# Layer 0's mixer in another order: keys and first queries before values, the last GLU pair after the fourth scores, and new planned waits

## The chip, the cores and the metric

The kernel runs on one core of a Trainium2 chip. The metric is device time of one launch, in microseconds; lower is better. It is given as the median of three runs. Beside it stands one profiled execution, from which all durations below are read.

## The reference

A decoder trunk of two layers over 512 tokens of width 1024, in float32. Each layer adds a token mixer and then a SwiGLU block to the residual, each behind an RMS norm. The change lies in layer 0's mixer, whose parts are these:

```
proj = h @ w_in                      # 1024 -> 1792: q (8 heads), k, v (2 heads), glu (2 x 512)
q, k = rotary(q), rotary(k)
a    = band_attention(q, k, v, window 127, sinks)        # 128-token blocks, own and previous block
c    = g_a * sigmoid(g_b)
c    = silu(layer_norm(causal_depthwise_conv(c, width 31)))
h    = h + concat(a, c) @ w_out
```

Layer 1's mixer (a dilated attention beside a spatial gating unit) and the two SwiGLU blocks keep their code; layer 1 shares two of the edited lines.

## The kernel before

Activations lie transposed, as eight tiles `xs[k]` of 128 channels by 512 tokens. Each float32 product is made of three TensorE (PE) matmuls of 128x512 on a high and a low half of both operands (`acc3`, L198 to L204). The halves of the weights are made on the fly: ScalarE (ACT) copies a tile's high half (`w_hi`, L174) and GpSimd (POOL) subtracts for the low half (`w_lo`, L151) while layer 0's mixer runs. Four such units are in flight, so POOL makes the next ones only as PE uses up the old ones.

**Steps.** The mixer is a list of steps, `C0["steps"]` (L40), that the loop at L681 walks: `k`, `v`, `q0` to `q3` are column tiles of the input projection, `gN` is a pair of them (`a` and `b`) for the GLU, `SN` and `VN` are scores and values of head pair N, `L` the convolution's layer norm. `A`, `X`, `Y`, `B`, `C` are pieces of the output projection: `A`, `X` and `Y` use attention tiles 0 to 3, `B0`, `B3` and `C12` use the four normed convolution tiles.

**PE's order is planned by hand.** `Seq` (L208) keeps a clock `seq.t`. Every `acc3` advances it by a fixed price (L204, L265). S, V and L are generators that yield (cost, wait); they are resumed between two `acc3` when their wait is over on that clock. So the numbers in `C0` (`q` before the first scores, `S` between halves of a score step, `ST` from scores to values, `TA` for a copy, `AO` for the normalised output, `ln` the clock time of the four transposes of the layer norm) set where in PE's stream each small step stands. PE runs that stream strictly in order; if an operand isn't there, all of PE waits. `seq.until` (L236) jumps the clock forward where a step has nothing left to run beside. The other engines' queues are ordered by the scheduler, and run in order too.

**GLU and convolution.** Once pair N is projected, VectorE (DVE) multiplies both halves (`glu`, L494), writing the padded tile `cp[N]` (`cp_124` to `cp_127` in the rows). Then `conv_tile` (L467) makes 31 taps: the first `taps[N]` go to POOL (ACT multiplies into `prod`, three buffers, L478; POOL adds into `yc`, L479), the others to DVE (L481, L483). A last DVE add joins both (L484). `yc_136` to `yc_139` are the four results.

**Layer norm.** `conv_norm` (L633) transposes each `yc` on PE into bank 7 (L641), takes statistics on DVE, then scales, transposes back (L668), applies Silu on ACT and splits in halves; only then `B0` can start.

**Scores and values.** `scores0` (L573) runs 16 small matmuls in two halves into banks 2 and 3; DVE masks and reduces (L598), ACT takes exponentials (L610). `values0` and `pt_av` (L620, L395) transpose the weights into banks 4 and 7, ACT copies them (`pts`, L410), PE multiplies by `Vt` (L421), DVE scales by `rl` (`on`, L430), PE transposes again (L435), and ACT and DVE split the result into `oh` and `ol` (L363, L364).

Of the kernel before, what the change touches and what calls it, by code (L numbers as in the profile page):

```python
# [10 lines left out]
def _warn_once_fixed(msg, *args, **kwargs):  # L11
# [13 lines left out]
S = 512  # L25
# [9 lines left out]
C0 = dict(  # L35

    first='a0 b0',
    steps='L g0 v q0 g1 k S0 q1 S1 V0 g2 q2 q3 S2 V1 g3 S3 V2 V3 A1 A0 A2 Y5 X1 A3 Y6 X3 X0 X2 Y7 B0 B3 C12',  # L40
    na=(0, 1), nx=(2, 3, 4),
    rope_v=('k', 'q2', 'q3'),
    taps=(8, 15, 15, 10),

    norm=(0.0, 2.6), q=5.99, v=0.5, S=3.13, ST=0.86, TA=0.65, AO=1.09, LB=4.85, LO=2.1, ln=(54.8, 69.91, 96.75, 112.86),

    n1=5, q1=6.6, S1=2.26, ST1=3.65, m1=11.78, M1=0.53, TA1=1.12, AO1=1.4,
)
# [86 lines left out]
def trunk_kernel(ctx: ExitStack, tc: tile.TileContext, xT, ws, cols, sinks, sgu_g, sgu_b,  # L135
# [11 lines left out]
    def bank(i, shape=None):  # L147
        return psum.tile(shape or [P, S], F32, name=f"bank{i}")
# [49 lines left out]
    def acc3(ps, x, start, stop):  # L198
        hi, lo = next_tile()
        xh, xl = x  # L200
        T.matmul(ps, hi, xh, start=start, stop=False)  # L201
        T.matmul(ps, hi, xl, start=False, stop=False)  # L202
        T.matmul(ps, lo, xh, start=False, stop=stop)  # L203
        seq.tick(0.648)  # L204

# [35 lines left out]
    seq = Seq()  # L243
# [7 lines left out]
    def tok_gemm(x, banks, each=None, hold=0, ready=None):  # L251

        ps = [bank(b) for b in banks]
        last = len(x) - 1

        def mac(t, k, row):
            hi, lo = row
            xh, xl = x[k]  # L260
            c = slice(t * P, (t + 1) * P)
            T.matmul(ps[t], xh[:, c], hi, start=(k == 0), stop=False)  # L262
            T.matmul(ps[t], xh[:, c], lo, start=False, stop=False)  # L263
            T.matmul(ps[t], xl[:, c], hi, start=False, stop=(k == last))  # L264
            seq.tick(0.648)  # L265

        for k in range(len(x) - hold):
            row = next_row()
            for t in range(NQ):
                mac(t, k, row)  # L270
            if each:
                each(k)
        if hold:
            rows = {k: next_row() for k in range(len(x) - hold, len(x))}
            for t in range(NQ):
                for k, row in rows.items():
                    mac(t, k, row)
                ready(t, ps[t])
        return ps
# [34 lines left out]
    norm = {}  # L314
# [80 lines left out]
    def pt_av(items, vap, rl, dst, banks, line="V", ta="TA", ao="AO"):  # L395

        po = bank(5, [P, 8, 64])
        turn = [0]

        def tbank():  # L400
            turn[0] += 1
            return bank(banks[turn[0] % len(banks)])

        def trans(grp):
            pt = tbank()
            for x, (u, pap, blk, first, last) in enumerate(grp):
                T.transpose(pt[:, x * P:(x + 1) * P], pap, ident)
            pts = mpool[0].tile([P, S], F32, name="pts", bufs=3)
            w = len(grp) * P
            A.activation(pts[:, :w], pt[:, :w], AF.Copy)  # L410
            return pts

        grps = [items[c:c + 4] for c in range(0, len(items), 4)]
        pts, at = {}, {}
        for g in range(min(2, len(grps))):
            pts[g] = trans(grps[g])
            at[g] = seq.t + 0.43 + C0[ta]
            yield 0.43, (0.0 if g == 0 else max(0.0, at[0] - seq.t - 0.43))
        for g, grp in enumerate(grps):
            for x, (u, pap, blk, first, last) in enumerate(grp):  # L420
                T.matmul(po[:, u, :], pts[g][:, x * P:(x + 1) * P], vap(u, blk), start=first, stop=last)  # L421
            cost = 0.43
            if g + 2 < len(grps):
                pts[g + 2] = trans(grps[g + 2])
                at[g + 2] = seq.t + 0.86 + C0[ta]
                cost = 0.86
            if g + 1 < len(grps):
                yield cost, max(0.0, at[g + 1] - seq.t - cost)
        on = mpool[0].tile([P, NQ, P], F32, name="on", bufs=1)
        V.tensor_mul(on.rearrange("p n (b e) -> p (n b) e", b=2), po,  # L430
                     rl[:, :, None].to_broadcast([P, 8, 64]))
        yield 0.43, C0[ao]
        pt = tbank()
        for n in range(NQ):
            T.transpose(pt[:, n * P:(n + 1) * P], on[:, n, :], ident)  # L435
        split(pt, oh_[0][dst], ol_[0][dst])
        done.add((line, dst))
        yield 0.43, 0.0
# [5 lines left out]
    with ExitStack() as mx:  # L444
# [126 lines left out]
        oh_[0], ol_[0] = oh, ol  # L571

        def scores0(i):  # L573
            yield 0.0, C0["q"]
            while i >= 2 and ("V", i - 2) not in done:
                yield 0.0, 0.3
            qss = qTs[i][1]
            Pm = mp.tile([P, 8, 2 * P], F32, name="Pm", bufs=2)
            nm = scr.tile([P, 8], F32, name="nm")
            l = scr.tile([P, 8], F32, name="l")  # L580
            for n2 in range(2):
                sb = [bank(2), bank(3)]
                for n1 in range(2):
                    n = 2 * n2 + n1
                    for b in range(2):
                        lo = max(n - 1, 0) * P
                        w = (n + 1) * P - lo
                        out = sb[b][:, n1 * 256 + 256 - w:n1 * 256 + 256]
                        q = slice(n * P, (n + 1) * P)
                        T.matmul(out, qss[b][:, q], khh[b][:, lo:lo + w], start=True, stop=False)  # L590
                        T.matmul(out, qss[b][:, q], kl[b][:, lo:lo + w], start=False, stop=True)
                for n1 in range(2):
                    n = 2 * n2 + n1
                    for b in range(2):
                        u = 2 * n + b
                        c0 = P if n == 0 else 0
                        hd = i + 4 * b
                        V.tensor_tensor_reduce(  # L598
                            out=Pm[:, u, c0:], in0=sb[b][:, n1 * 256 + c0:n1 * 256 + 256],
                            in1=mask0[:, c0:], scale=-0.125, scalar=nsink[:, hd:hd + 1],  # L600
                            op0=ALU.add, op1=ALU.min, accum_out=nm[:, u:u + 1])
                if n2 == 0:
                    yield 0.9, C0["S"]
            es = scr.tile([P, 8], F32, name="es")
            V.tensor_tensor(out=es.rearrange("p (n b) -> p n b", b=2),
                            in0=nm.rearrange("p (n b) -> p n b", b=2),
                            in1=sinkb[:, i:i + 5:4][:, None, :].to_broadcast([P, NQ, 2]), op=ALU.add)
            for u in range(8):
                c0 = P if u < 2 else 0
                A.activation(Pm[:, u, c0:], Pm[:, u, c0:], AF.Exp, bias=nm[:, u:u + 1], scale=-1.0,  # L610
                             accum_out=l[:, u:u + 1])
            A.activation(es, es, AF.Exp)
            rl = scr.tile([P, 8], F32, name="rl")
            V.tensor_add(rl, l, es)
            V.reciprocal(rl, rl)
            del qTs[i]
            pend[i] = Pm, rl, seq.t + 0.9 + C0["ST"]
            yield 0.9, 0.0

        def values0(i):  # L620
            while i not in pend:
                yield 0.0, 0.3
            Pm, rl, at = pend.pop(i)
            yield 0.0, max(0.0, at - seq.t)
            items = []
            for u in range(8):
                n, b = divmod(u, 2)
                if n:
                    items.append((u, Pm[:, u, 0:P], n - 1, True, False))
                items.append((u, Pm[:, u, P:], n, n == 0, True))  # L630
            yield from pt_av(items, lambda u, blk: Vt[:, blk, 64 * (u % 2):64 * (u % 2) + 64], rl, i, (4, 7))

        def conv_norm():  # L633

# [1 line left out]
            bs = scr.tile([P, NQ, 4, 6], F32, name="bs")  # L636
            for j in range(4):
                yield 0.0, max(0.0, C0["ln"][j] - seq.t)
                pt = bank(7)
                for t in range(NQ):  # L640
                    T.transpose(pt[:, t * P:(t + 1) * P], yc[j][:, t * P:(t + 1) * P], ident)  # L641
                for t in range(NQ):
                    V.bn_stats(bs[:, t, j, :], pt[:, t * P:(t + 1) * P])
                A.activation(y[:, :, j * P:(j + 1) * P], pt.rearrange("p (t c) -> p t c", t=NQ), AF.Copy)
                yield 0.43, 0.0
# [32 lines left out]
                yield 0.43, (C0["LO"] if 0 < j < 3 else 0.0)  # L678

        qTs, pend, po, ks, early = {}, {}, {}, {}, {}  # L680
        for step in C0["steps"].split():  # L681
            kind, i = step[0], int(step[1:] or 0)
            if kind == "g":
# [658 lines left out]
```

## Time and profile before

| | |
|---|---|
| median of three runs | 1114.96 us (1112.4 to 1115.18) |
| profiled execution | 1111.7 us |
| span of its instructions | 1110.0 us |
| PE busy over the span | 1069.4 us (96%) |
| DVE, ACT, POOL busy | 694.0, 571.6, 233.2 us |

Layer 0's mixer takes the first 200 us or so. A timeline row reads: start, duration, engine, line, operation, output and inputs, count, and in brackets the idle time just before it with what ended it. Busy time of PE counts overlapping matmuls; the pace of dense 128x512 matmuls is read from the starts.

### The profile page before, as it was taken

To read this page: it belongs to the slowest core of one execution; us is meant where nothing else is said; L and a number is where in the kernel's file an instruction comes from. 1 tells how busy PE (TensorE), PEld (TensorE's weight loads), DVE (VectorE), ACT (ScalarE), POOL (GpSimd) and SP (SyncE) were. 2 spreads that over 40 slices of the span, in tenths; PEclk is the share of its full clock that TensorE was granted. 3 is DMA by queue.
4 is the path that set the end of the run, shared out by engine and by line. 5 is a ranking of instruction groups with operands and counts; after the bars stand their busy time and mean duration, and the time that the engine had idled before them with its cause. 6 is when DMAs were issued, how large, how long until landed. Compare 5 with 4: busy or idle time off the path is not lost.

```text
span 1110.0 us, 13707 instructions
## 1 busy us (share of the span) xinstructions
PE 1069.4 (96%) x5118; PEld 886.8 (80%) x5118; DVE 694.0 (63%) x1059; ACT 571.6 (51%) x930; POOL 233.2 (21%) x210
## 2 busy tenths in 40 slices
PE   9988889999999999999999999999899999999997
PEld 7767777878888888888887888888788888888785
DVE  3899965876565655564748646666765646555543
ACT  6577756754445353543637654446544443535433
POOL 0799744211101010100024200002110110101002
PEclk9999899999999999999999999999999999999999
DMA  6221112987757676621522112239877676766112
GB/s 228 68 76 58 39 38 76 285 210 192 181 160 169 181 150 198 144 47 57 160 98 83 41 43 72 77 106 269 207 194 188 154 172 185 140 197 143 29 67 76
DMA packets 42803, 145.89 MB, mean 131 GB/s; under 512 B 4848, under 2 KB 5744, under 8 KB 42736
## 3 DMA queue, kind: packets, MB, share of 16 engines
q1 hardware_dynamic: 30496, 100.88, 26.4%
q0 software_dynamic: 11520, 41.95, 22.3%
q10 hardware_dynamic: 720, 2.18, 0.6%
q8 instruction: 40, 0.66, 0.2%
q14 instruction: 27, 0.22, 0.1%
HBM read 142.89 MB, written 2.10 MB: 131 GB/s over the span
## 4 chain that ended last, share of the span: by engine, by line
PE 77%; DVE 10%; DMA 4%; ACT 4%; issue 3%; POOL 2%; POOLq 0%; ACTq 0%; DVEq 0%
PE bank L201 11%; PE bank L202 10%; PE bank L907 10%; PE bank L203 10%; PE bank L908 10%; PE bank L905 10%; DMA raw<-in_ws 4%; PE bank L262 2%; PE bank L264 2%; PE bank L263 2%; DVE bank L483 2%; PE bank L421 2%; PE bank L920 1%; DVE w2l L151 1%; ACT w2h L881 1%
## 5 line engine op out<-in xcount | busy, mean ns | idle before, releaser
L151 DVE TENSOR_TENSOR w2l<-raw,w2h 128x1024 fp32r<-128x1024 f32 x140 | 171.2, 1225 | 204.8 <-ACT w2h L881 200.5
L881 ACT ACTIVATE w2h<-raw 128x1024 fp32r<-128x1024 f32 x140 | 147.8, 1059 | 210.8 <-PE bank L908 159.0
L174 ACT ACTIVATE w_hi<-raw 128x512 fp32r<-128x512 f32 x204 | 127.7, 628 | 178.3 <-PE bank L202 141.2
L871 POOL DMA_DIRECT2D raw<-in_ws x80 | 69.6, 876 | 551.6 <-DVE w2l L151 229.7
L151 DVE TENSOR_TENSOR w_lo<-raw,w_hi 128x512 fp32r<-128x512 f32 x164 | 115.9, 710 | 57.1 <-ACT w_hi L174 57.0
L907 PE MATMUL bank<-w2l,s 128*128 128x512 f32 x320 | 125.0, 391 | 2.7 <-DVE w2l L151 2.7
L905 PE MATMUL bank<-w2h,s 128*128 128x512 f32 x320 | 125.6, 393 | 1.5 <-DVE gb L841 1.3
L908 PE MATMUL bank<-w2h,s 128*128 128x512 f32 x320 | 124.7, 390 | 0.0
L201 PE MATMUL bank<-xh,w_hi 128*128 128x512 f32 x272 | 110.0, 404 | 1.1 <-ACT w_hi L174 1.1
L203 PE MATMUL bank<-xh,w_lo 128*128 128x512 f32 x272 | 106.8, 393 | 0.0
L202 PE MATMUL bank<-xl,w_hi 128*128 128x512 f32 x272 | 106.7, 392 | 0.0
L201 PE MATMUL bank<-hh,w_hi 128*128 128x512 f32 x256 | 99.8, 390 | 0.0
L202 PE MATMUL bank<-hl,w_hi 128*128 128x512 f32 x256 | 99.7, 390 | 0.0
L203 PE MATMUL bank<-hh,w_lo 128*128 128x512 f32 x256 | 99.7, 389 | 0.0
L905 PE MATMUL bank<-w2h,xh 128*128 128x512 f32 x240 | 94.4, 393 | 0.0
L908 PE MATMUL bank<-w2h,xl 128*128 128x512 f32 x240 | 93.5, 390 | 0.0
L907 PE MATMUL bank<-w2l,xh 128*128 128x512 f32 x240 | 93.4, 389 | 0.0
L907 PEld LDWEIGHTS bank<-w2l,s 128*128 128x128 f32 x320 | 60.1, 188 | 16.3 <-DVE w2l L151 4.1
L905 PEld LDWEIGHTS bank<-w2h,s 128*128 128x128 f32 x320 | 60.1, 188 | 15.0 <-DVE gb L841 1.7
L908 PEld LDWEIGHTS bank<-w2h,s 128*128 128x128 f32 x320 | 60.1, 188 | 12.5
L151 POOL TENSOR_TENSOR w_lo<-raw,w_hi 128x512 fp32r<-128x512 f32 x40 | 54.8, 1371 | 58.5 <-ACT w_hi L174 56.0
L479 POOL TENSOR_TENSOR yc<-yc,prod 128x512 f32<-128x512 f32 x44 | 60.6, 1377 | 10.9 <-ACT prod L478 9.5
(237 smaller groups left out, 2056.1 us busy)
## 6 DMA issues: line engine op xcount, KB each, us to landing
raw<-in_ws SPq DMA_DIRECT2D x177, 512.0 KB, 4.3
raw<-in_ws POOLq DMA_DIRECT2D x80, 512.0 KB, 5.7
h<-in_xT SPq DMA_DIRECT2D x8, 256.0 KB, 5.6
raw<-in_ws ACTq DMA_DIRECT2D x4, 512.0 KB, 5.1
out_y<-xh SPq DMA_DIRECT2D x4, 256.0 KB, 2.0
out_y<-xl SPq DMA_DIRECT2D x4, 256.0 KB, 2.3
raw<-in_ws SPq DMA_DIRECT2D x2, 256.0 KB, 4.0
ropeC<-in_rope_c SPq DMA_DIRECT2D x2, 256.0 KB, 4.1
```

The costliest lines, as they stand in the source:

```text
L151: eng.tensor_tensor(out=out, in0=a, in1=b, op=ALU.subtract)
L174: A.activation(hi, src, AF.Copy)
L201: T.matmul(ps, hi, xh, start=start, stop=False)
L202: T.matmul(ps, hi, xl, start=False, stop=False)
L203: T.matmul(ps, lo, xh, start=False, stop=stop)
L262: T.matmul(ps[t], xh[:, c], hi, start=(k == 0), stop=False)
L479: G.tensor_add(yc[j], yc[j], p)
L871: nc.gpsimd.dma_start(t, ws[base + 8 * (g - 1) + 2 * BLOCK_OF[more] + q], accum_op=ALU.add)
L881: A.activation(hi, src, AF.Copy)
L905: T.matmul(ps[t], xh[:, c], wh[:, w], start=(start and j == 0), stop=False, skip_group_check=True)
L907: T.matmul(ps[t], xh[:, c], wl[:, w], start=False, stop=False, skip_group_check=True)
L908: T.matmul(ps[t], xl[:, c], wh[:, w], start=False, stop=(j == 3), skip_group_check=True)
```

## The change

The step list is reordered: `k` and `q0` are projected before `v`; the two tiles of `g1` stand on both sides of the first half of S0; V1 moves before S2 and V2 before S3; `g3`, the last GLU pair, comes after S3 in the list, so its projection runs beside S3 and V2. Tile 3 of the convolution gives POOL 14 instead of 10 of the first taps. The planner's price of an `acc3` rises from 0.648 to 0.682, the waits get new numbers, one per head pair for `q`. Values and layer norm keep out of each other's way (`busy`, `quiet`, `LS`), and the banks of the transposes in `pt_av` are taken from the first of the list on.

```
-    steps='L g0 v q0 g1 k S0 q1 S1 V0 g2 q2 q3 S2 V1 g3 S3 V2 V3 A1 A0 A2 Y5 X1 A3 Y6 X3 X0 X2 Y7 B0 B3 C12',
+    steps='L g0 k q0 v S0 g1 q1 V0 S1 g2 q2 V1 S2 q3 V2 S3 g3 V3 A0 A1 A2 Y5 X0 X1 A3 Y6 X3 X2 Y7 B0 B3 C12',
...
-    taps=(8, 15, 15, 10),
-
-    norm=(0.0, 2.6), q=5.99, v=0.5, S=3.13, ST=0.86, TA=0.65, AO=1.09, LB=4.85, LO=2.1, ln=(54.8, 69.91, 96.75, 112.86),
+    taps=(8, 15, 15, 14),
+
+    norm=(0.0, 2.6), q=(11.0, 7.0, 7.0, 6.0), v=1.2, S=3.13, ST=3.0, TA=0.9, AO=2.4, LB=4.85, LO=2.1, LS=3.5, ln=(60.0, 84.0, 114.0, 134.0),
...
-        seq.tick(0.648)
+        seq.tick(0.682)
...
-            return bank(banks[turn[0] % len(banks)])
+            return bank(banks[(turn[0] - 1) % len(banks)])
...
-            yield 0.0, C0["q"]
+            yield 0.0, C0["q"][i]
...
+            while seq.t < quiet[0]:
+                yield 0.0, 0.3
+            busy.append(i)
...
+            busy.remove(i)
...
+                while busy:
+                    yield 0.0, 0.3
+                quiet[0] = seq.t + C0["LS"]
                 pt = bank(7)
...
+        busy, quiet = [], [0.0]
```

On PE, the transposes of the last convolution tile (`yc_139`) stood in the middle of the output projection (a piece of `Y6`, bank 1559):

```order
L201 MATMUL bank_1559<-oh_313,w_hi 128x512
L202 MATMUL bank_1559<-ol_321,w_hi 128x512
L203 MATMUL bank_1559<-oh_313,w_lo 128x512
L641 MATMUL bank_1572<-ident,yc_139 128x128 x4
L201 MATMUL bank_1559<-oh_314,w_hi 128x512
L202 MATMUL bank_1559<-ol_322,w_hi 128x512
L203 MATMUL bank_1559<-oh_314,w_lo 128x512
```

Now they stand behind the last matmul of `Y7` (bank 1625), the transposes back (`yn`) follow at once, and then `B0`, the first matmuls on a normed convolution tile (`oh_316`):

```order
L201 MATMUL bank_1625<-oh_315,w_hi 128x512
L202 MATMUL bank_1625<-ol_323,w_hi 128x512
L203 MATMUL bank_1625<-oh_315,w_lo 128x512
L648 MATMUL bank_1644<-ident,yc_139 128x128 x4
L675 MATMUL bank_1671<-ident,yn 128x128 x4
L675 MATMUL bank_1681<-ident,yn 128x128 x4
L201 MATMUL bank_1434<-oh_316,w_hi 128x512
L202 MATMUL bank_1434<-yc_1676,w_hi 128x512
```

The 24 matmuls of the output projection that stood between the two kinds of transposes, and 21 more between the second kind and `B0`, have moved ahead of both.

On DVE, the multiply that makes the last GLU tile (`cp_127`) stood right behind the reductions of the third scores S2 (the `nm` and `es` rows end it):

```order
L598 ISA nm 128x1
L483 SCALAR_TENSOR_TENSOR bank_914<-cp_126,cc,bank_914 128x512
L605 TENSOR_TENSOR es<-nm,sinkb 128x8
L614 TENSOR_TENSOR rl<-l,es 128x8
L615 RECIPROCAL rl<-rl 128x8
L498 TENSOR_TENSOR gb<-bank_1211,R 128x512
L484 TENSOR_TENSOR yc_138<-yc_138,bank_914 128x512
L502 SCALAR_TENSOR_TENSOR cp_127<-gb,ga 128x512
L481 TENSOR_SCALAR bank_1280<-cp_127,cc 128x512
L483 SCALAR_TENSOR_TENSOR bank_1280<-cp_127,cc,bank_1280 128x512 x10
```

Now it stands behind those of the fourth scores S3, and behind the output of V2 (`on` and `ol_322`):

```order
L598 ISA nm 128x1
L605 TENSOR_TENSOR es<-nm,sinkb 128x8
L614 TENSOR_TENSOR rl<-l,es 128x8
L615 RECIPROCAL rl<-rl 128x8
L498 TENSOR_TENSOR gb<-bank_1239,R 128x512
L364 TENSOR_TENSOR ol_322<-bank_1359,oh_314 128x512
L502 SCALAR_TENSOR_TENSOR cp_127<-gb,ga 128x512
L481 TENSOR_SCALAR bank_1375<-cp_127,cc 128x512
L483 SCALAR_TENSOR_TENSOR bank_1375<-cp_127,cc,bank_1375 128x512 x8
```

All of S3's eight reductions and one more `on` and `ol` have moved ahead of `cp_127`, and none of the 55 taps of tiles 0 to 2 has moved behind it.

On POOL, the adds into the last convolution tile (`yc_139`) were nine, with one weight half between them:

```order
L479 TENSOR_TENSOR yc_139<-yc_139,prod 128x512 x6
L151 TENSOR_TENSOR w_lo<-raw,w_hi 128x512
L479 TENSOR_TENSOR yc_139<-yc_139,prod 128x512 x3
L151 TENSOR_TENSOR w_lo<-raw,w_hi 128x512
L751 TENSOR_TENSOR h_77<-h_77,qT 128x512
```

Now they are thirteen: five, then eight single ones among eight weight halves and three adds into the residual (`h_77` to `h_79`). The last rows of that stretch are these:

```order
L759 TENSOR_TENSOR h_78<-h_78,qT 128x512
L479 TENSOR_TENSOR yc_139<-yc_139,prod 128x512
L151 TENSOR_TENSOR w_lo<-raw,w_hi 128x512 x2
L479 TENSOR_TENSOR yc_139<-yc_139,prod 128x512
L151 TENSOR_TENSOR w_lo<-raw,w_hi 128x512
L759 TENSOR_TENSOR h_79<-h_79,qT 128x512
L479 TENSOR_TENSOR yc_139<-yc_139,prod 128x512
```

The last add of `yc_139` has moved behind the residual add of `Y7`.

## Rows read from the trace of the kernel before

**Rows 1.** Windows: stretch, length, busy of PE, PEld, DVE, ACT, POOL; PE clock, DMA.

```profile
31.30:128.60 97.30, 84.40 (x428) 70.06 (x427) 93.36 (x173) 67.66 (x142) 85.06 (x62) 0.96 0.19 60
153.00:182.00 29.00, 28.91 (x136) 23.18 (x135) 9.96 (x19) 15.09 (x23) 17.11 (x13) 1.00 0.23 73
```

**Rows 2.** Waits of PE, 0 to 240 us: total, times, longest.

```profile
PE bank L435 <- DVE on L430: 4.0, 3, 1.9
PE bank L407 <- ACT yn L644: 3.8, 2, 2.8
```

**Rows 3.** Waits of DVE, 31.3 to 128.6 us.

```profile
DVE ga L501 <- PE bank L203: 1.7, 2, 1.4
```

**Rows 4.** Groups by form, DVE, 31.3 to 128.6 us: busy, mean ns.

```profile
L717 DVE TENSOR_TENSOR qs<-qT,qs 64x512 fp32r<-64x512 f32 x8 | 8.5, 1066 | 0.2
L502 DVE SCALAR_TENSOR_TENSOR cp<-gb,ga 128x512 f32<-128x512 f32 x4 | 4.0, 1008 | 0.1
L605 DVE TENSOR_TENSOR es<-nm,sinkb 128x8 f32<-128x8 f32 x3 | 3.4, 1126 | 0.0
L614 DVE TENSOR_TENSOR rl<-l,es 128x8 f32<-128x8 f32 x3 | 2.3, 752 | 0.3 <-ACT es L612 0.3
```

**Rows 5.** Groups by form, DVE, 128.6 to 152 us.

```profile
L598 DVE CUSTOM_DVE_ANT_0 Pm<-bank,mask,nsink 128x256 f32<-128x256 f32 x6 | 2.6, 478 | 0.0
L430 DVE TENSOR_TENSOR on<-bank,rl 128x512 f32<-128x512 f32 x2 | 1.4, 688 | 0.8 <-PE bank L421 0.8
L598 DVE CUSTOM_DVE_ANT_0 Pm<-bank,mask,nsink 128x128 f32<-128x128 f32 x2 | 0.7, 348 | 0.6 <-PE bank L591 0.6
```

**Rows 6.** Timeline of DVE: start, duration, instruction.

```profile
31.30 0.69 DVE L384 TENSOR_TENSOR ropeC<-ropeC,R 128x512 f32<-128x512 f32 x1 [5.55 <-ACT R L359]
...
112.62 0.69 DVE L717 TENSOR_TENSOR qs<-qT,qs 64x512 fp32r<-64x512 f32 x1
...
127.89 0.69 DVE L502 SCALAR_TENSOR_TENSOR cp<-gb,ga 128x512 f32<-128x512 f32 x1
...
129.41 7.88 DVE L483 SCALAR_TENSOR_TENSOR bank<-cp,cc,bank 128x512 f32<-128x512 f32 x10
...
147.84 0.16 DVE L605 TENSOR_TENSOR es<-nm,sinkb 128x8 f32<-128x8 f32 x1
```

**Rows 7.** Timeline of POOL.

```profile
61.52 1.74 POOL L479 TENSOR_TENSOR yc<-yc,prod 128x512 f32<-128x512 f32 x1
...
130.73 8.05 POOL L479 TENSOR_TENSOR yc<-yc,prod 128x512 f32<-128x512 f32 x6 [2.90 <-ACT prod L478]
...
163.94 1.31 POOL L751 TENSOR_TENSOR h<-h,qT 128x512 f32<-128x512 f32 x1
165.19 1.32 POOL L151 TENSOR_TENSOR w_lo<-raw,w_hi 128x512 fp32r<-128x512 f32 x1
```

**Rows 8.** Timeline of PE, the last transposes, and the start of `B0`.

```profile
160.61 0.60 PE L641 MATMUL bank<-ident,yc 128*128 128x128 f32 x4
...
172.93 0.39 PE L203 MATMUL bank<-oh,w_lo 128*128 128x512 f32 x1
173.16 0.39 PE L201 MATMUL bank<-oh,w_hi 128*128 128x512 f32 x1
```

**Rows 9.** Timeline of ACT in the layer norm's tail.

```profile
168.72 1.45 ACT L671 ACTIVATE ga<-bank,cc 128x512 f32<-128x512 f32 x2
170.06 0.63 ACT L363 ACTIVATE oh<-ga 128x512 fp32r<-128x512 f32 x1
```

**Rows 10.** Timeline of PE behind its longest wait for `kl`.

```profile
68.00 0.38 PE L591 MATMUL bank<-kl,qs 128*128 128x128 f32 x1 [2.48 <-DVE kl L698]
...
69.15 0.63 PE L201 MATMUL bank<-xh,w_hi 128*128 128x512 f32 x1
...
71.28 0.52 PE L203 MATMUL bank<-xh,w_lo 128*128 128x512 f32 x1
```

**Rows 11.** Waits of PE in layer 1's mixer.

```profile
PE bank L1145 <- DVE st L1124: 2.0, 1, 2.0
```

More of the change, by code (lines that the diff above doesn't have):

```diff
@@ L264, in mac @@
             T.matmul(ps[t], xl[:, c], hi, start=False, stop=(k == last))
-            seq.tick(0.648)
+            seq.tick(0.682)
         for k in range(len(x) - hold):
```

## The prediction

> **What bounds the kernel now.** I read the windows of layer 0's mixer first, then who waited for whom, then the groups of DVE in the busiest stretch, then the timelines around the last convolution tile. Over the whole run PE looks like the bound, and from 153 us to 182 us it is, busy for 28.91 of 29 us [rows 1]. Between 31.3 and 128.6 us it isn't: DVE is busy for 93.36 of 97.30 us there, POOL for 85.06, PE for 84.40 [rows 1]. PE's longest waits in the mixer are waits for this chain, such as 4.0 us for the output `on` on DVE and 3.8 us for ACT's copy `yn`, which itself follows DVE's statistics [rows 2]. DVE in turn waited 1.7 us for PE in its largest such group [rows 3]. So up to 128.6 us, where the last GLU tile `cp_127` is written [rows 6], DVE's queue sets the pace, and PE's gaps are slack. Afterwards the last convolution tile goes through POOL, DVE and the layer norm, hidden behind PE's output projection: the transposes of `yc_139` are at 160.61 us, and PE has matmuls without a gap until `B0` at 173.16 us [rows 8].
>
> So I follow one date, the end of `cp_127`, and then the way from there to `B0`.
>
> **Step 1: the front of the mixer, no gain by itself.** With `k` and `q0` ahead of `v`, 99 matmuls of the projection lie between the keys and the first scores instead of 33, and PE's 2.48 us wait there goes [rows 10]. The new waits `ST`, `AO` and the `busy`/`quiet` pair should shorten the waits for `on` and `yn`, at most 7.8 us together [rows 2]. I cost these at nothing: PE arrives earlier at things that DVE delivers in its own time, and would wait at the next of them.
>
> **Step 2: when `cp_127` is ready.** All taps of tiles 0 to 2 stay ahead of it on DVE, and so do the ropes, the halves and three scores. Added ahead of it are S3's eight reductions, 2.6 + 0.7 = 3.3 us, and V2's `on` and `ol`, twice 0.69 us, `ol` taken at the row of `on` [rows 5]. S3's `es` and `rl` and its reciprocal come to 0.5 us at 0.16 us each, the short form in the row at 147.84 us [rows 6], and to some 2.1 us at the means of 1126 and 752 ns [rows 4]. I take the short form, since POOL's adds for tile 2 are nearly over there; sum 5.2 us. The tables are scaled one `acc3` earlier (0.7 us). So +4.5 us: 128.58 becomes 133.1 us.
>
> This rests on DVE's other work taking as long as before. Instructions with two operands in SBUF are stretched: the eight `qs` subtractions average 1066 ns against 0.69 us for the shortest row, the `cp` multiplies 1008 against 0.69, `es` 1126 and `rl` 752 against 0.16 us once POOL is quiet [rows 4, 6]. That is 8 x 0.38 + 4 x 0.32 + 3 x 0.97 + 3 x 0.59, some 9.0 us. POOL's work ahead of this point is the same (the same 35 adds, rope halves and weight halves), so I keep the stretch. Both ends: all 9.0 us gone gives -4.5 us, the long forms of `es` and `rl` give +6.1 us.
>
> The Trainium skill (SBUF — State Buffer, section "Who interferes with whom") says that a DVE instruction with two SBUF inputs and a GpSimd instruction that reads SBUF exclude each other for a whole instruction, so a stretched instruction is not slower, it stands behind POOL. The trace agrees: the 128x8 `es` takes 0.16 us beside an idle POOL and 1126 ns on the mean beside a busy one. By that rule the stretch stays while POOL is as busy as before, and the sum stands; without it, the early end above would be as likely as any.
>
> **Step 3: from `cp_127` to the transposes of `yc_139`.** Before, this took 160.61 - 128.58 = 32.0 us, of which a good part was planned waiting: DVE's ten-tap run is at 0.79 us a tap, POOL's first six adds at 1.34 us each [rows 6, 7]. Now POOL has 13 adds, and between them eight weight halves and three residual adds, 24 instructions in a row. The first add follows `cp_127` by 2.15 us, as before (130.73 - 128.58) [rows 6, 7]. Five adds at 1.34 us are 6.7 us, 19 more at 1.25 us (the distance of the two rows at 163.94 and 165.19 us) 23.8 us [rows 7]. With the joining add on DVE, taken at 0.69 us like `on` [rows 5], the sum is 33.3 us: +1.3 us. DVE's share, 17 taps at 0.79, is done after 14 us and no longer matters. PE's own work from there to the end of `Y7` is 32 `acc3` of 0.68 us (0.227 us a matmul, rows 8) and V3, some 26 us, so PE stands idle for about 7 us in front of these transposes. If each of the 24 took the 1.74 us of a blocked add [rows 7], it would be 9.7 us more; with POOL behind its adds only, 13 x 1.34 us, 13 us less, but then PE's 26 us and the residual add of `Y7` ahead of the last tap hold it at 30 us. Both ends: -2 and +11 us.
>
> **Step 4: the layer norm is bare.** Before, 12.55 us passed from these transposes to `B0`, covered by 45 matmuls. Now nothing is left to cover it; `seq.until` jumps. The first high half `oh` was ready at 170.69 us, 10.1 us after the transposes [rows 8, 9]. One Silu of 0.73 us stood in front of it that now stands behind it, and a weight copy, taken at the 0.63 us of the copy of `oh` [rows 9]. I take 9 us, so `B0` comes 3.5 us sooner behind the transposes than before. Ends: 7.8 us (if a small DVE step there isn't blocked by POOL) and the old 12.55 us.
>
> **Step 5: after `B0`.** PE will have idled for some 15 us in two gaps. Behind the 2.48 us wait the matmuls from 69.15 to 71.28 us started 0.43 us apart instead of 0.23, the lower of the clock's two levels [rows 8, 10]; five of them cost 1.0 us. I take 1.6 us. `B3` needs the low half of the last normed tile, two Silus, two copies and a subtraction behind the first high half, 4 to 5 us against the 3.4 us of `B0`: 1.0 us. One more group of transposes back stands behind `B0`'s start: 0.4 us. Together +3.0 us (0.4 to 5).
>
> **Step 6: layer 1.** The higher price of an `acc3` makes its planner move the first scores one `acc3` earlier. They waited 2.0 us for DVE's `st` there [rows 11], so they now wait 0.7 us longer. The other steps stand where they stood, but for a few single `acc3`. The new order of the banks touches no wait that I can name.
>
> **Sum.** +4.5 + 1.3 - 3.5 + 3.0 + 0.7 = +6.0 us. On the profiled execution's 1111.7 us that is 1117.7; that execution lies 3.3 us under the median of the runs, 1114.96, so I forecast 1121 us for the median.
>
> **Rivals.**
> (a) PE and its waits are the bound, or DVE's stretch is mostly chance. For it: 7.8 us in two groups of PE's waits [rows 2], and an order in which PE asks for each thing later, so that DVE's small steps meet POOL less often. Against it: DVE's 96% in that stretch. Its mechanism is `cp_127` coming early; the sum breaks even where it is 6.0 us earlier than forecast, near 127 us. With most of the 9.0 us gone it is 125 us, and the time about -2 to -4 us: 1112. Faster.
> (b) The front gains about as much as the tail loses: `cp_127` at the old 128.6 us, the rest as worked out, +1.5 us, 1116.5. For it: half of the stretch would do it. Against it: five microseconds of named work moved ahead of that multiply.
> (c) POOL is the bound outright: its adds run blocked in the tail as at 61.52 us for half of the 24, +5.9 us on top, 1127. For it: DVE's taps read SBUF beside it. Against it: six adds ran at 1.34 us beside ten such taps [rows 6, 7].
> (d) The change doesn't do what it says: the planned clock and the chip drift apart, and V2 and S3 beside `g3` make PE wait in its projection. That is inside step 2 as long as DVE is later than PE; beyond, it ends as (c).
>
> **How the numbers follow.** My forecast has 0.52, (a) 0.18, (b) 0.23, (c) with (d) 0.07. A measurement of this kernel tells about 0.3%, 3.3 us, from no change: faster is under 1111.6, slower over 1118.3. The forecast's own range, 1117 to 1125, is slower but for its lowest part (0.05), (b) is within but for a sixth. Faster 0.18, same 0.25, slower 0.57. The range for 8 in 10 takes in (a)'s middle and the lower half of (c): 1112 to 1127.
>
> **What would show it.** Right: the fourth `cp` multiply ends near 133 us; POOL without a gap from there on; the four transposes of `yc_139` some 33 us later, with a PE wait of 5 to 8 us in front of them that names DVE's joining add; another wait of about 5 us in front of the transposes back, with `yn` as its reason; `B0` near 175 us. The PE waits on `on`, `kl` and `yn` in the front are smaller, and yet the date of `cp_127` is not earlier. Wrong: `cp_127` before 127 us, or less than 8 us of PE idle time between `Y7` and `B0`.

## The result, and the profile after

The changed kernel takes 1123.42 us (median of 4 runs, 1121.60 to 1124.71) against 1114.94 for the kernel before: a ratio of 1.0079, 95% interval 1.0062 to 1.0096, 8.5 us slower. Its profiled execution took 1123.45 us, its span is 1121.8 us. That is 11.8 us more than the span of the execution profiled before, which lay 3.3 us under its own median.

| date in the trace, us | before | after | difference |
|---|---|---|---|
| end of `cp_127` on DVE | 128.58 | 137.51 | +8.9 |
| transposes of `yc_139` on PE | 160.61 | 170.90 | +10.3 |
| first matmul of `B0` | 173.16 | 179.40 | +6.2 |
| first norm matmul of layer 0's FFN (line 341) | 206.87 | 217.77 | +10.9 |
| first state matmul of layer 1 (weight load) | 586.1 | 596.7 | +10.6 |
| last state matmul of layer 1 (weight load) | 660.1 | 672.0 | +11.9 |

The windows of the changed kernel, columns as in [rows 1]; the third stretch holds PE's idle time and what follows it:

```profile
31.30:128.60 97.30, 85.55 (x444) 71.79 (x443) 92.50 (x179) 68.43 (x150) 81.61 (x60) 0.95 0.19 60
153.00:182.00 29.00, 18.24 (x73) 13.71 (x72) 6.12 (x20) 11.98 (x18) 18.15 (x15) 0.79 0.16 55
165.00:195.00 30.00, 17.49 (x67) 12.69 (x66) 8.01 (x21) 11.51 (x17) 9.94 (x9) 0.77 0.15 51
```

The first stretch looks as before: DVE 92.5 of 97.3 us, PE a little busier. The second has turned over: PE 18.24 us of 29 where it had 28.91 [rows 1], at a mean granted clock of 0.79 instead of 1.00.

PE's five largest waits, 0 to 250 us: total, times, longest.

```profile
PE bank L648 <- DVE yc L484: 5.6, 1, 5.6
PE bank L421 <- ACT pts L410: 5.1, 4, 2.1
PE bank L590 <- DVE qs L725: 4.7, 4, 2.6
PE bank L675 <- ACT yn L669: 3.9, 1, 3.9
PE bank L407 <- ACT yn L651: 2.5, 1, 2.5
```

The waits on `on` [rows 2] and on `kl` [rows 10] are gone from the top. In their place stand waits on `qs` (the rotated queries) and `pts` (the copied weights), and two new ones in the tail, on `yc` and on the normed `yn` (line 675).

DVE around the end of `cp_127`, and at its join of the last tile (start, duration, instruction, wait and its releaser):

```profile
127.30 0.69 DVE L484 TENSOR_TENSOR yc<-yc,bank 128x512 f32<-128x512 f32 x1
130.97 0.69 DVE L430 TENSOR_TENSOR on<-bank,rl 128x512 f32<-128x512 f32 x1 [2.98 <-PE bank L421]
...
135.19 0.69 DVE L498 TENSOR_TENSOR gb<-bank,R 128x512 f32<-128x512 f32 x1 [0.31 <-PE bank L203]
135.80 0.68 DVE L364 TENSOR_TENSOR ol<-bank,oh 128x512 fp32r<-128x512 f32 x1
136.58 0.93 DVE L502 SCALAR_TENSOR_TENSOR cp<-gb,ga 128x512 f32<-128x512 f32 x1
...
170.15 0.69 DVE L484 TENSOR_TENSOR yc<-yc,bank 128x512 f32<-128x512 f32 x1 [12.87 <-POOL yc L479]
```

This is what the forecast did not have: DVE has run dry in front of `on` (3.0 us) and again in front of `gb` (0.3 us), both times for PE. `gb` is the first step behind `g3`'s projection. So PE's queue, not DVE's, hands over late. The window up to the end of `cp_127`, to set beside the first of [rows 1]:

```profile
31.30:137.51 106.21, 93.67 (x493) 78.65 (x492) 97.66 (x194) 73.45 (x165) 84.17 (x62) 0.95 0.17 55
```

DVE has 4.3 us more work up to that date and 4.6 us more idle time (8.6 instead of 3.9 us). PE itself waited in front of the second half of that projection, for the layer norm's copy `yn` and then for `qs`:

```profile
119.82 0.66 PE L407 MATMUL bank<-ident,Pm 128*128 128x128 f32 x4 [2.50 <-ACT yn L651]
...
122.56 0.47 PE L590 MATMUL bank<-khh,qs 128*128 128x128 f32 x1 [1.24 <-DVE qs L725]
```

POOL from `cp_127` on, beginning and end:

```profile
139.41 6.74 POOL L479 TENSOR_TENSOR yc<-yc,prod 128x512 f32<-128x512 f32 x5 [2.45 <-ACT prod L478]
...
167.64 1.26 POOL L759 TENSOR_TENSOR h<-h,qT 128x512 f32<-128x512 f32 x1
168.86 1.26 POOL L479 TENSOR_TENSOR yc<-yc,prod 128x512 f32<-128x512 f32 x1
```

And PE behind it, where [rows 8] had matmuls without a gap:

```profile
170.90 1.11 PE L648 MATMUL bank<-ident,yc 128*128 128x128 f32 x4 [5.59 <-DVE yc L484]
175.94 2.25 PE L675 MATMUL bank<-ident,yn 128*128 128x128 f32 x8 [3.94 <-ACT yn L669]
179.40 0.80 PE L201 MATMUL bank<-oh,w_hi 128*128 128x512 f32 x1 [1.21 <-ACT oh L363]
...
187.71 0.50 PE L201 MATMUL bank<-oh,w_hi 128*128 128x512 f32 x1 [1.53 <-DVE oh L680]
```

### The profile page after: what moved, and what is told of

It reads as the page before. It is cut to its first block, busy times and chain, and to the rows that moved or that the text cites. A ratio compares the mean times of both kernels' runs of the same rounds, so it can differ in the third digit from the quotient of the medians.

```text
span 1121.8 us, 13720 instructions
## 1 busy us (share of the span) xinstructions
PE 1071.8 (96%) x5118; PEld 889.0 (79%) x5118; DVE 688.5 (61%) x1055; ACT 573.4 (51%) x934; POOL 237.6 (21%) x214
## 4 chain that ended last, share of the span: by engine, by line
PE 69%; DVE 5%; DMA 4%; ACT 3%; issue 2%; POOL 1%; POOLq 0%; ACTq 0%; DVEq 0%
PE bank L916 10%; PE bank L915 10%; PE bank L913 10%; PE bank L201 9%; PE bank L202 9%; PE bank L203 9%; DMA raw<-in_ws 4%; PE bank L262 2%; PE bank L264 2%; PE bank L263 2%; PE bank L421 2%; DVE w2l L151 1%; PE bank L928 1%; ACT w2h L889 1%; PE bank L407 1%
## 5 line engine op out<-in xcount | busy, mean ns | idle before, releaser
L479 POOL TENSOR_TENSOR yc<-yc,prod 128x512 f32<-128x512 f32 x48 | 65.2, 1359 | 5.2 <-ACT prod L478 3.7
```

What stands on the lines that cost most here:

```text
L479: G.tensor_add(yc[j], yc[j], p)
```

## The experiments

Eleven kernels and the kernel before once more, each profiled and timed in three rounds. The kernel before ran beside them at medians of 1115.2 to 1115.3 us, so their times can be set side by side. Theory A is that of the prediction.

**10 taps and 4 taps on POOL: the tail.** The edit to the changed kernel, and the same with 4:

```diff
-    taps=(8, 15, 15, 14),
+    taps=(8, 15, 15, 10),
```

> The changed kernel with 10 instead of 14 of tile 3's first taps on POOL; PE's order is the same. Theory A (behind cp_127 the tail is one chain: POOL's adds into yc_139, then the layer norm with nothing beside it): the nine adds end before PE has finished Y7, the 5.6 us wait in front of the last transposes goes, the layer norm stays bare, so 5.5 us less than the changed kernel, about 1118 us. Theory B (the time was lost further ahead, in PE's waits on qs, pts and yn around V1, V2 and S3, and the wait at the tail only absorbs it): the front is the same, so within 1 us of the changed kernel, 1123.

> The changed kernel with 4 of tile 3's taps on POOL, 27 on DVE. Theory A: with ten taps the chain had already fallen behind PE's Y7, so six fewer bring nothing more: 5 to 6 us less than the changed kernel, within 1 us of the run with ten, although POOL has six adds (8 us) less. If POOL itself were the bound all the way, it would be another 5 us faster than with ten. Theory B: 1123 us.

With 10 taps 1117.58 us (1114.50 to 1120.79), with 4 taps 1118.13 us. Both ratios to before are 1.0024 (1.0008 to 1.0040, and 1.0009 to 1.0039). With 10 taps:

```profile
164.74 0.60 PE L648 MATMUL bank<-ident,yc 128*128 128x128 f32 x4
170.26 2.25 PE L675 MATMUL bank<-ident,yn 128*128 128x128 f32 x8 [4.92 <-ACT yn L669]
173.72 0.80 PE L201 MATMUL bank<-oh,w_hi 128*128 128x512 f32 x1 [1.21 <-ACT oh L363]
```

The transposes no longer wait, and the 5.8 us that come back are the 5.59 us wait. Fewer taps than 10 give nothing more, since PE itself arrives at 164.7. `cp_127` ended at 135.51 here: it is late, but it makes PE wait no longer at the transposes once POOL has less to do behind it.

**DVE's work left out.** Four of DVE's taps in each of tiles 0 to 2 (ahead of `cp_127`), and in a second kernel 12 of tile 3 (behind it):

```diff
-                for t in range(TAPS):
+                for t in range(TAPS - (4 if j < 3 else 0)):
```

> The changed kernel without the last four DVE taps of tiles 0, 1 and 2 (12 taps of 0.75 us are left out, so the convolution is incomplete). Theory A (DVE's queue sets when cp_127 is ready): cp_127 comes 5 to 9 us earlier and the whole time falls by as much, to 1114 to 1118 us, although nothing of the tail is changed. Theory B in the form that PE's own waits set the front: cp_127 moves by less than 2 us and the time stays at 1121 to 1123.

> The changed kernel without the last 12 DVE taps of tile 3 (left out, so the convolution is incomplete): as much DVE work as in the run with four taps fewer in tiles 0 to 2, but behind cp_127. Theory A: DVE has been waiting 12.9 us for POOL there, so nothing changes, 1122.5 to 1124 us. If DVE's total work in the mixer were the bound, it would be 5 to 9 us faster, like the other one.

1123.4 us (ratio 1.0076, 1.0052 to 1.0100) and 1124.63 us (1.0082, 1.0059 to 1.0105): neither moves. For tile 3 that was expected. For the front it refutes theory A. `cp_127` ended at 136.38, 1.1 us earlier, for some 9 us less work on the engine that was to set its date. That gain is inside the scatter: in five profiles of the same front (the changed kernel, 10 taps, 4 taps, tile 3's taps left out, and layer 1's price below) it ended between 135.5 and 138.7 us. The window and DVE's waits of that run:

```profile
31.30:128.60 97.30, 87.87 (x452) 73.99 (x450) 83.93 (x167) 69.73 (x152) 82.42 (x61) 0.93 0.18 60
```

```profile
DVE on L430 <- PE bank L421: 5.4, 1, 5.4
...
DVE ra L390 <- PE bank L203: 2.5, 1, 2.5
DVE gb L498 <- PE bank L203: 1.7, 2, 1.4
```

The work that went (92.50 to 83.93 us busy) turned into waiting for PE. So PE's order was tried next (theory B), and POOL as the one behind PE's waits on `qs` (theory C).

**POOL's work left out in the front.**

```diff
-                        G.tensor_add(yc[j], yc[j], p)
+                        if j == 3 or t > 4:
+                            G.tensor_add(yc[j], yc[j], p)
```

> The changed kernel with the first four of GpSimd's additions left out in the convolution of tiles 0, 1 and 2 (12 additions, about 1.3 us each, some 16 us of GpSimd's time before g3; ScalarE still makes the products, VectorE's part is whole). The convolution's sum is incomplete in those tiles. Theory B (TensorE's in-order stream sets the end of g3: V2 and S3 stand ahead of it, with their waits on pts, qs and yn): cp_127 ends within 1.5 us of 137.5, the waits on qs stay at 4 to 5 us, the time is 1122 to 1125. Theory C (GpSimd, 82 of 97 us busy, makes the rotated queries late, and that makes TensorE wait on qs and g3 late): the waits on qs shrink to 1 us or less, cp_127 ends 3 us or more earlier, and the time falls with it to 1120 or below.

1122.68 us (1.0068, 1.0045 to 1.0092). The waits on `qs` nearly went, as C said. `cp_127` ended at 134.54, 3.0 us earlier than in the changed kernel's profile, but only 1.0 us under the earliest of the five with the same front, so a gain of 3 us isn't shown. PE then waited for `pts`:

```profile
PE bank L421 <- ACT pts L410: 7.2, 2, 4.1
PE bank L591 <- DVE qs L726: 1.1, 2, 0.8
```

And POOL's chain behind `cp_127` took 34.9 us instead of 33.4, since it then waited for weight copies of ACT. PE's wait of 5.6 us on `yc` stayed.

**`g3` ahead of `q3`, `V2` and `S3`.**

```diff
-... V1 S2 q3 V2 S3 g3 V3 ...
+... V1 S2 g3 q3 V2 S3 V3 ...
```

> The changed kernel with the last GLU pair g3 projected ahead of q3, V2 and S3 and not behind them; taps (14 for tile 3) and the late layer norm stay. Theory B: the last matmul of g3 no longer stands behind V2 (its wait of 2.5 us on yn with it), S3 and q3, so cp_127 ends at 125 to 130 instead of 137.5, GpSimd's chain of 33.4 us behind it ends at 159 to 163, before TensorE's own stream is through at about 165, the wait of 5.6 us on yc goes, and the time is 1116 to 1119, as with 10 taps in run e1_taps10. Theory C or any other theory in which a supplier paces the front whatever the order: cp_127 ends at 135 or later and the time is 1121 to 1124.

1122.46 us (1.0056, 1.0033 to 1.0079): B is right on the date, wrong on the time. `cp_127` ended at 119.35 (the `cp` row starts at 118.27), 18 us earlier. The window up to there:

```profile
31.30:119.35 88.05, 80.98 (x420) 67.32 (x418) 84.93 (x165) 64.75 (x139) 78.93 (x59) 0.98 0.18 63
```

The edit moved DVE's work too: 84.93 us of it stand ahead of `cp_127` where 97.66 stood, and DVE is now idle for only 3.1 us of 88. So the 18 us are not PE's alone. That PE's order holds the date in the changed kernel rests on this run together with the one in which DVE's work was left out ahead of it. What holds PE is in part open: its waits from 30 to 138 us add up to 12.6 us of 108 there, on `qs`, `pts` and `yn` above all. PE's wait on `yc` went too. But the transposes came at 168.99. Windows at and behind the place that `g3` left:

```profile
118.00:136.00 18.00, 13.08 (x81) 10.81 (x80) 17.03 (x30) 13.72 (x28) 17.69 (x13) 0.97 0.18 59
135.00:150.00 15.00, 12.69 (x60) 11.36 (x59) 12.40 (x25) 7.99 (x19) 8.96 (x8) 0.62 0.00 0
```

Without `g3`'s matmuls between them, the scores and values stand one behind the other and wait for ACT and DVE (2.3 us), at a granted clock of 0.62 from 135 to 150 us. PE lost there what POOL gave back: at this place of its stream it is 4.3 us later than with 10 taps.

**The late layer norm alone, in the kernel before.**

```diff
-... ln=(54.8, 69.91, 96.75, 112.86),
+... ln=(54.8, 69.91, 96.75, 134.0),
```

> The kernel before with nothing changed but the planned time of the last transposes of the layer norm (112.86 to 134), which puts them behind the last matmul of Y7 as in the changed kernel: 45 matmuls that stood between these transposes and the first of B0 (10.2 us at 0.227 us) now stand ahead of them. TensorE had no gap in the 8 us ahead of these transposes. Theory: the transposes move from 160.6 to about 170.8, the distance from them to B0 falls from 12.55 to 8.5 us, B0 comes at 179.3 instead of 173.2, and the time is 1119 to 1122 (+6). Rival, step 4 taken by itself (a shorter distance is a gain): 1111 to 1113.

1127.69 us (1124.59 to 1134.71; ratio 1.0126, 1.0081 to 1.0171): the direction as expected, twice the size (the two shortest of the four runs, 1124.6, lie 9.3 us above the kernel before). The profiled execution (1134.71) is the longest of its runs, and some 6.5 us of it arise before the edit has any effect, most of them in one instruction (last section): the transposes of V3's `on` stand at 159.04 instead of 152.54 us. Net of that the transposes are at 172.5 us. From the transposes to the FFN's first norm matmul it takes 48.0 us, against 46.3 in the kernel before, although 45 matmuls (10.2 us) fewer lie in between. The distance to `B0` is 9.0 us instead of 12.55, and all of that is lost again behind `B0`: the granted clock is 0.66 from 180 to 195 us. A bare layer norm saves nothing; the matmuls put in front of it are paid in full.

**Cover again.** The changed kernel, with the last transposes back in front of 42 matmuls:

```diff
-    taps=(8, 15, 15, 14),
+    taps=(8, 15, 15, 8),
-... ln=(60.0, 84.0, 114.0, 134.0),
+... ln=(60.0, 84.0, 104.0, 114.0),
```

> The changed kernel with 8 instead of 14 of tile 3's taps on ScalarE and GpSimd, and the planned times of the last two of the layer norm's transposes at 104 and 114 instead of 114 and 134: the last ones then stand in front of 42 matmuls of Y7 and its neighbours, as in the kernel before. Theory: in run e1_taps10 TensorE came to the last transposes at 164.7 without waiting for them, so it is at their new place at 164.7 - 42 x 0.227 = 155.2; yc_139 is ready there or within 2 us; B0 comes at 165 to 168 instead of 173.7, and the time is 1108 to 1112, faster than the kernel before by 3 to 6 us: the new order of the front was worth about 5 us and the bare layer norm hid it. Rival (step 1 as predicted, the front order worth nothing on TensorE's stream, VectorE late): yc_139 comes at 160 or later, B0 at 171 or later, time 1114 to 1117.

1112.31 us (1110.18 to 1113.50; ratio 0.9973, 0.9955 to 0.9990), 5.3 us less than with 10 taps and the bare norm. The transposes stood at 159.39 behind a wait of 2.98 us; PE was there at 156.4, 1.2 us later than reckoned. `B0` came at 172.39 us, not at 165 to 168, so the gain of 3 us is the least of what was expected.

**The old front on top of that.**

```diff
-    steps='L g0 k q0 v S0 g1 q1 V0 S1 g2 q2 V1 ...
+    steps='L g0 v q0 g1 k S0 q1 S1 V0 g2 q2 V1 ...
```

> The kernel of run e10_covered_norm (8 taps, layer norm covered, 1112.3 us) with the front of the kernel before put back: values and the second GLU pair projected ahead of keys and the second queries, S0 behind k and V0 behind q1. Theory (the new front is worth 3 to 5 us on TensorE's stream, since e10_covered_norm is 3.0 us faster than the kernel before with the same place of the last transposes): the wait on kl of 2 to 4 us at the first scores is back, and the time is 1115 to 1118. Rival (step 1 as predicted, front waits worth nothing because what follows waits for VectorE or GpSimd anyway): 1111 to 1113.5.

1111.35 us (1106.32 to 1113.71; ratio 0.9955, 0.9931 to 0.9978), no slower than with the new front. My theory of a gain from the front fails, and the rival, the prediction's step 1, holds: keys first is worth nothing here. The wait on `kl` did not come back either; with the new planned waits kept, PE waited 5.5 us for `ol` and 3.2 us for `rb` instead, 12.6 us in all from 30 to 140 us against 11.8 with the new front. So the 3 us by which the covered kernel beats the one before come from something else that the two share (8 taps, the order from `V1` on, the planned waits). The kernel under "Together" rules out the 8 taps; which of the others it is was not tried.

**Layer 1's price.** In the changed kernel the planner's cost goes back to the old one from layer 1 on:

```diff
-        seq.tick(0.682)
+        seq.tick(TK[0])
...
-    ffn(0, "od_g")
+    ffn(0, "od_g"); TK[0] = 0.648
```

> The changed kernel with the planner's cost of three matmuls put back from 0.682 to 0.648 from layer 1 on, and nothing else. Theory (step 6): the wait on st in layer 1 falls from 2.7 to 2.0 us, the distance from the first to the last of the state matmuls from 75.4 to about 74.2 us, the time to 1122 to 1123. Rival: what is longer in layer 1 is only the half clock of that execution, and the distance stays above 75.

1124.59 us (1.0082, 1.0058 to 1.0105); a microsecond can't be told at this spread. The trace shows it. The state matmuls' weight loads in this run and, under it, PE's wait:

```profile
L1153 PEld LDWEIGHTS bank<-st x32: 186/188/192, 595.7 to 669.7; 128*128 128x128 f32 x32
```

```profile
PE bank L1153 <- DVE st L1132: 2.0, 1, 2.0
```

That is 74.0 us. In the changed kernel it is 75.3 with a wait of 2.7. Over all profiles, the old cost gave 73.9 to 74.0 five times out of five, the new one 75.3 to 75.4 in seven of nine and 73.8 in two. The extra 1.3 us goes with a lower clock: 0.96 from 600 to 640 us in the changed kernel, 1.00 in this one. In the two at 73.8 us the wait is 2.7 us as well and the clock 1.00 from 580 to 670 us; PE's waits on `pts` are 0.8 us shorter there than with the old cost (1.5 against 2.3). So the longer wait by itself costs nothing; what costs is the lower clock behind it.

**Together.** 10 taps, the covered norm and the old cost from layer 1 on:

> The kernel of run e10_covered_norm with 10 taps instead of 8 on ScalarE and GpSimd (in e10_covered_norm VectorE's own taps ended last, at 158.5, 2 taps of 0.79 us less for it) and the planner's old cost from layer 1 on. Theory: the wait of 3.0 us on yc at the last transposes falls to 1.5 or less, layer 1 gives about 1 us back, and the time is 1109 to 1111. Rival: the end is set elsewhere by now, 1112 to 1113.

1108.12 us (1106.97 to 1111.66; ratio 0.9927, 0.9901 to 0.9954): 7.2 us faster than the kernel before and 15.3 faster than the changed one, more than expected. With the taps of the kernel before (10) and its place of the last transposes, the rest of the change is a gain. Against the kernel with 10 taps and the bare norm it is 9.5 us, of which layer 1's price can be 1.3. PE on the way:

```profile
155.40 0.63 PE L648 MATMUL bank<-ident,yc 128*128 128x128 f32 x4 [1.47 <-DVE yc L484]
161.37 1.24 PE L675 MATMUL bank<-ident,yn 128*128 128x128 f32 x8
```

**The kernel before once more.**

> The kernel before, unchanged, profiled once more. In run e9_before_bare_norm a subtraction of VectorE (qs, 64x512, at 49.27 us) took 5.99 us where the same instruction at the same place took 1.02 us in the profile of before, while GpSimd ran five operations on SBUF without a gap, and everything behind it came about 5 us later. Theory (two vector engines share the way to SBUF, and which gets it first is a matter of some ns, so the same program has several times): if this execution is 3 us or more above 1111.7, one or two of VectorE's operations with two inputs in SBUF are longer by as much. Rival: such an operation never takes over 1.7 us in this kernel, and a longer execution shows its time elsewhere.

1116.10 us (ratio 1.0014, 0.9988 to 1.0041), the profiled execution 1114.46. It came 2.8 us above the first one, short of the 3 us named, and no such instruction took over 1.7 us: the rival holds for this execution. It shows how far dates of one program move: `cp_127` at 132.44 instead of 128.58, the transposes at 163.40 instead of 160.61. Of that 1.2 us are there at the first `cp` multiply (35.48 instead of 34.31).

## Why the prediction was right, and where it wasn't

The time was right: 1123.4 us in a range of 1112 to 1127, with 1121 as the value, and slower as the likeliest sign. Not all of its reasons were, and that the median came within 2.4 us owes something to luck: between the profiled executions 6.0 us were forecast and 11.8 measured, and the 3.3 us by which the first of them was under its median took much of that back.

- **Step 1, the front is worth nothing: right,** as the old front on the covered kernel shows (1111.35 against 1112.31 us). The reason given, that PE would wait for DVE at the next thing, is right only in part: the next waits are on `qs`, which DVE makes, and on `pts`, which ACT makes.
- **Step 2, `cp_127` 4.5 us later: wrong in its reason, its size in doubt.** It was 8.9 us later than in the first execution and 5.1 later than in the second, and profiles of the same front differ by 3.2 us. DVE's work was priced well, 4.3 us more up to this date; the 4.6 us of added idle time the step put at nothing. The step that failed is "DVE's queue sets the pace" up to that date, as a premise for the changed order. Taking 9 us out of this queue gained 1.1 us of the date, inside the scatter, and nothing of the time; moving `g3` in PE's queue gained 18 us of it, with 12.7 us of DVE's work moved behind it as well. What I had set aside as rival (d), `V2` and `S3` making PE wait in `g3`'s projection, is what happened, and DVE waited there. It did not end as (c), as (d) had it: POOL's adds ran unblocked, and the time is 1123.4, not 1127. For the kernel before the premise fits what two odd executions show (last section): a subtraction of DVE that took 5 us longer put `cp_127` 7.6 us later in the old order (its second execution was 3.9 later without one), while in the order with `V1` ahead of `S2` and `g3` last a block as long left it at 138.24 us, beside 138.25 without one.
- **Step 3, from there to the transposes 33.3 us: right.** 33.39 us, POOL nearly without a gap, PE's wait 5.6 us where 5 to 8 were named. With 10 taps the wait and 5.8 us went. When `cp_127` came earlier (POOL lightened), the chain stretched to 34.9 us, so the date moves less than `cp_127`. The upper end of this step was added up wrongly, without touching the forecast: 24 instructions at 1.74 us are 41.8 us, 11.3 more than the 30.5 priced and not 9.7, so that end is +12.6.
- **Steps 4 and 5, the bare norm -3.5 and +3.0: both mis-sized, the sum off by 1.1 us.** To `B0` 8.5 us, so -4.05; behind it +4.7, with the clock at 0.87 from 180 to 195 us and waits on the normed tiles. From the transposes to the FFN it is 46.87 us against 46.26: +0.6 where I had -0.5.
- **Step 6, +0.7: measured +1.3, for another reason.** The wait on `st` is 0.7 us longer as said, but two profiles with that wait took no longer than the old cost (73.8 us). The 1.3 us are a stretch at the lower clock, which I had not foreseen.
- **The sum** +6.0 became +11.8 on the profiled executions: +8.9 + 1.4 + 0.6 + 1.3, and -0.4 in the rest of the program. By medians it is +8.5, since the execution I forecast from lay 3.3 us under its median.

What the sum hid is the larger point. POOL's four extra taps cost 5.8 us. The uncovered norm costs 5.3 us measured with two more taps on POOL (10 against 8), and up to 9.5 with 10 taps on both sides and layer 1's old price on one. Together that is more than 8.5, because the rest of the change gains: 3.0 us in the covered kernel, 7.2 in the last one, which has the taps and the layer 1 price of the kernel before. While POOL holds the transposes back, PE has idle time for the matmuls in front of them, and the bare norm looks free, as in my steps 3 to 5. Once POOL is relieved, it is the next thing that costs.

## What to carry to other kernels

An engine that is 95% busy over a stretch need not set its end. Look at the last date of the stretch, whom the instruction there waited for, and test it by taking work out of the engine that you suspect; then compare the date with its scatter over several profiles. When cover is moved from behind a latency to in front of it, measure both orders between two dates that lie outside. And profile the kernel before twice: its own dates moved by 2.8 to 3.9 us between two executions, as much as most terms of this sum.

## What the runs showed of the hardware

Which of DVE and POOL gets to SBUF first can decide microseconds. Up to 49.27 us the kernel before and the same with the late norm issue the same instructions, and the dates compared differ by 10 to 30 ns. Then, DVE in the kernel before:

```profile
49.26 1.02 DVE L717 TENSOR_TENSOR qs<-qT,qs 64x512 fp32r<-64x512 f32 x1
50.20 0.74 DVE L483 SCALAR_TENSOR_TENSOR bank<-cp,cc,bank 128x512 f32<-128x512 f32 x1
```

with the late norm:

```profile
49.27 5.99 DVE L717 TENSOR_TENSOR qs<-qT,qs 64x512 fp32r<-64x512 f32 x1
55.19 0.74 DVE L483 SCALAR_TENSOR_TENSOR bank<-cp,cc,bank 128x512 f32<-128x512 f32 x1
```

and POOL in that run:

```profile
48.39 1.34 POOL L151 TENSOR_TENSOR w_lo<-raw,w_hi 128x512 fp32r<-128x512 f32 x1
49.65 1.33 POOL L479 TENSOR_TENSOR yc<-yc,prod 128x512 f32<-128x512 f32 x1
50.90 2.58 POOL L151 TENSOR_TENSOR w_lo<-raw,w_hi 128x512 fp32r<-128x512 f32 x2
53.39 1.33 POOL L479 TENSOR_TENSOR yc<-yc,prod 128x512 f32<-128x512 f32 x1
57.92 1.29 POOL L151 TENSOR_TENSOR w_lo<-raw,w_hi 128x512 fp32r<-128x512 f32 x1 [3.19 <-ACT w_hi L174]
```

The subtraction ends only when POOL's run without a gap is over, at 54.72 us, four instructions behind the one that ran when it began. The Trainium skill (SBUF — State Buffer, section "Who interferes with whom") says that the pair of ports that the two engines share is an exclusive lock, and that the order of issue decides who blocks. The trace agrees, and goes further: the loser can lose four turns in a row, where in the kernel before the two took turns (the two `qs` subtractions took 1.02 and 1.54 us, POOL's add at 49.62 us 1.81 instead of 1.33). With the old front on the covered kernel it happened once more (5.61 us at 50.28 us), and that execution was as short as its neighbours, 1112.32 us. In one of the two executions the block moved all that followed, in the other nothing; that it costs only where DVE sets the pace would fit both, but no run was made to show it.
